# The first DeltaNet triangular solve in pinned pieces inside the attention, its row steps on GpSimd; weight splits pinned one projection ahead

## The chip, the cores and the metric

The kernel runs on one core of a Trainium2 chip. The metric is the device time of one execution in microseconds (us); for the kernel before, the median of three runs is 1260.77 us (1259.69 to 1261.77). The core's engines are TensorE (PE, matrix products, PEld its weight loads), VectorE (DVE), ScalarE (ACT), GpSimd (POOL) and SyncE (SP), whose queue issues the DMAs. Each works through its own instructions in order and waits on semaphores for the others.

## The reference

One layer of a hybrid transformer on 512 latent tokens with 256 context tokens, width 1024, in float32. One input projection feeds two branches, which are gated, merged, projected and followed by a gated MLP:

```python
attn_x = latent_attention(q_x, k_all, v_all)          # 8 query heads, 2 key heads, 768 keys
gdn_x_in = gdn_prepare(qkv_x, db_x, da_x, conv_qkv_w, a_log, dt_bias)   # conv, silu, l2 norm, rates
o_x, o_c = gdn_bidirectional(gdn_c_in, gdn_x_in, update_ctx)            # 8 heads, both directions
gdn_x = gdn_output(o_x, z_x, gdn_norm_w)
x = x + g1 * merge_branches(attn_x, gdn_x, gate_x, w_pa, w_pd, w_out)
x = x + g2 * conv_ffn(modulate(rms_norm(x), sh2, sc2), w_up, ffn_conv_w, ffn_conv_b, w_down)
```

The change is in the DeltaNet branch. In each chunk of 64 tokens it solves a triangular system per head and direction:

```python
a_mat = jnp.where(strict, beta[..., :, None] * dec * kk, 0.0) + jnp.eye(GDN_CHUNK)
uw = lax.linalg.triangular_solve(a_mat, rhs, left_side=True, lower=True, unit_diagonal=True)
```

Here kk are the products of keys with keys, dec the decays between two tokens and beta a rate per token. The kernel inverts a_mat: first its diagonal blocks of 32 by substitution, then larger blocks by products.

## The kernel before, in words

**Products.** A float32 matrix is split into a high and a low part (`split`: ACT writes whi, DVE writes wlo = wraw - whi, L121), and a product is three matmuls (hi·hi, hi·lo, lo·hi; `mm3`, L125). A weight block is fetched by `load_w` (L200): a DMA on SP into wraw (128x1024), then its split.

**Stages.** Up to 75 us the modulation vectors. To about 153 us the attention's q, k and v columns: `pq` in PSUM, rotary steps on DVE (qt, qtmp), transposes `pt`. Then the attention (`attend`, L824): 32 units, each a head with 128 queries. A unit's scores go to the PSUM tile pS; DVE takes the maximum (mx, a TENSOR_REDUCE), ACT the exponential (pm), DVE normalises, PE transposes pm into the bank ab, ACT and DVE split that into PH and PL, and PE multiplies with the values. PE's waits in a unit are filled with steps of the DeltaNet input projections (`projections`, L419: matmuls mb, taps t1 and output co on ACT and DVE, transposes xb). From 326.86 us DeltaNet is done for four pairs of heads, while what is left of the projections, the gates and the attention's output projection serves as filler (`filler`, L1201). What of the filler is left behind the last scan runs then; the output projection, up and down follow.

**DeltaNet of a pair.** `gdn_prep` (L875) loads the keys kT and, broadcast from DRAM, decays (NN and Gb), adds a mask (768 columns at a time) and takes 24 exponentials on ACT. `gdn_solve` (L903) multiplies 12 products of keys (bank pk) into NN, collects the diagonal blocks by transposes and ACT copies into C, transposes C into X, scales it with the rates gT and does the substitution: for each of 31 rows one product (prod) and one addition into R. `gdn_solved` (L940) scales R by gT and transposes it into o_tr and o_nt. `gdn_inv` (L952) begins with products pb of o_tr and o_nt with NN and builds the inverse T (tiles TTm, Tm), `gdn_scan` (L1020) runs over the chunks; its first matmul is pb with vtok. rkk and hk are inverse norms of keys and values; each of the eight heads has one rsqrt for each on GpSimd.

**What sets the order.** The scheduler orders each engine by priority (`first`, `sooner`, `solver`, `early`, L141 to 151); `keep_in_program_order` pins an instruction to its place in the program. PE's are pinned in this part, so no matmul passes another that waits. How much filler lies between DeltaNet steps is set by counts: `weave(g, rate)` takes `rate` steps of filler for each step of g, `wait(n)` is n steps with no DeltaNet work. WK = 24 steps stand ahead of the first solve, W0 = 66 behind it; `both(inv, solve)` weaves the next pair's solve into an inversion. The first solve runs on DVE, the other three on GpSimd (SPOOL).

Of the kernel before, what the change touches and what calls it, by code (L numbers as in the profile page):

```python
# [31 lines left out]
CHUNK, WK, W0, W1, RI, RS, RO = 1, 24, 66, 0, 3.0, 2.8, 2.0  # L32
# [34 lines left out]
RA = .6  # L67
F0, F1, F2, F3 = 3, 1, 1, 1
# [9 lines left out]
def hybrid_layer_body(tc, x, ctxt, xT, consts, cols, rows, w_mod1, w_mod2, w_av, w_aq, w_cm, w_pa, w_pd, w_out,  # L78
# [26 lines left out]

    def tt(out, a, b, op, eng=None):
        (eng or V).tensor_tensor(out=out, in0=a, in1=b, op=op)  # L107

    def ts(out, a, s1, op0, s2=None, op1=None, eng=None):
        if op1 is None:  # L110
            (eng or V).tensor_scalar(out=out, in0=a, scalar1=s1, scalar2=None, op0=op0)
        else:
            (eng or V).tensor_scalar(out=out, in0=a, scalar1=s1, scalar2=s2, op0=op0, op1=op1)  # L113

    def stt(out, a, s, b, op0, op1):
        V.scalar_tensor_tensor(out=out, in0=a, scalar=s, in1=b, op0=op0, op1=op1)  # L116

    def act(out, a, f=AF.Copy, **kw):
        A.activation(out, a, f, **kw)  # L119
# [13 lines left out]
    with es:  # L133
# [89 lines left out]
        vtd = [dp.tile([P, NA], F32, name=f"vtd{i}") for i in range(NH)]  # L223
        szd = [dp.tile([P, NL], F32, name=f"szd{i}") for i in range(NH)]
# [54 lines left out]
        def conv_proj(tile_idx, out, with_ctx):  # L279
            w = load_w(w_cm[tile_idx])  # L280
# [58 lines left out]
        def head_proj(h, part):  # L339
            o = cbuf()  # L340
            yield from conv_proj(8 * part + h, o, part != 0)
            head_out(h, part, o)
# [325 lines left out]
        QH = [ap_.tile([P, 2, NL], F32R, name=f"QH{i}") for i in range(4)]  # L668
        QL = [ap_.tile([P, 2, NL], F32R, name=f"QL{i}") for i in range(4)]
        kv_es = ExitStack()  # L670
        with kv_es:
# [27 lines left out]

            pend, dec = [], decays(kvp)  # L700
            pinned[0] = KPIN
            psc = next(dec)
            for blk in range(6):
# [5 lines left out]
                for t in range(6 if blk < 2 else 4):  # L709
# [10 lines left out]
                    if len(pend) >= LAG:  # L720
                        columns(*pend.pop(0))
# [27 lines left out]
                if blk > 1:  # L749
# [10 lines left out]
        with at_es:  # L760
# [13 lines left out]
            def abank():  # L774
                return aps.tile([P, 512], F32, name="ab", tag="ab", bufs=NB - 2)

            hold = {}
# [33 lines left out]
            def softmax(h, t, pS):  # L811
# [3 lines left out]
                with sooner():  # L815
                    V.tensor_reduce(out=mx[:, 0:1], in_=pS[:, 0:NA], axis=AX.X, op=ALU.max)
                    stt(mx[:, 1:2], mx[:, 0:1], -1.0, sc, ALU.mult, ALU.mult)
                    act(pm, pS[:, 0:NA], AF.Exp, scale=sc, bias=mx[:, 1:2], accum_out=mx[:, 2:3])
                with first():
# [3 lines left out]

            def attend():  # L824
                U = 4 * NH
                at = lambda u: (u // 4, u % 4)
                pS, pms, pv = scores(0, 0), {}, None
                yield F0
                for u in range(U + 2):
                    if u < U:  # L830
                        pms[u] = softmax(*at(u), pS)
                    if u + 1 < U:
                        pS = scores(*at(u + 1))
                    yield F1
# [360 lines left out]

        with early():
            pre = gdn_prep(0, V if P0 else G)
# [3 lines left out]
        def filler():  # L1201
# [4 lines left out]
            for h in range(NH):  # L1206
                yield from head_proj(h, 0)
                ready.append(h)
                yield from z_proj(h)
# [109 lines left out]
        weave(gdn_solve(pre, G if 0 in SPOOL else V), RK)  # L1319
        gdn_solved(pre, False)  # L1320
# [8 lines left out]
        for p in range(NP):  # L1329
            cur = pre  # L1330
            pre = gdn_prep(p + 1) if p + 1 < NP else None
            g = stage(p, cur, pre)
            weave(g, RI if p else RI0)
# [275 lines left out]
```

## Time and profile before

| | us |
|---|---|
| median of three runs | 1260.77 |
| profiled execution | 1257.86 |
| its span, first to last instruction | 1256.0 |
| attention's first scores | 156.27 |
| filler behind the attention begins | 326.86 |
| first inversion (pb<-o_tr) | 420.06 |
| first matmul of scan 0 (pb<-vtok) | 447.95 |
| second inversion | 511.61 |

The 1.86 us between execution and span lie outside the first and last instruction. Times of the profile are counted from the span's start. A row names the engine, the line of the kernel (often that of a helper), the operation, the output and input tiles with their sizes, how many it groups, and the busy time; in brackets or behind the last bar stands the idle time before it and what ended it.

### The profile page before, as it was taken

The numbers are of one execution on the slowest core, as the hardware profiler recorded it, in microseconds if no ns is written. First come the engines' busy times: TensorE is split into PE (matmuls) and PEld (weight loads), VectorE is DVE, ScalarE is ACT, GpSimd is POOL, SyncE is SP. The second block draws the span as 40 slices with busy tenths as digits, with TensorE's granted clock in tenths as the row PEclk, the third lists the DMA queues.
The fourth block names the chain that finished last, engine by engine and source line by source line (L and its number), as shares of the span: only waits on it lengthen the run. The fifth ranks groups of instructions, "written<-read, shape, count | busy, mean of one in ns | idle before, by whom it ended". The sixth has DMA issues, their size and how long they took to land.

```text
span 1256.0 us, 20509 instructions
## 1 busy us (share of the span) xinstructions
PE 1194.4 (95%) x7733; PEld 1016.6 (81%) x7733; DVE 837.5 (67%) x1609; ACT 613.3 (49%) x1403; POOL 274.3 (22%) x347
## 2 busy tenths in 40 slices
PE   6999999999888899999999999999999999999996
PEld 3499879898777778778888678789888888888886
DVE  5766767777688867775757688855776756653333
ACT  6534466666675673673643622333544444442231
POOL 0020110110432488587484200210000000000000
PEclk9999999999999999999999999999999999999998
DMA  9312211211634443543536786764343333223331
GB/s 381 140 59 85 88 58 59 81 59 68 201 110 171 159 134 114 165 155 105 173 135 193 241 288 198 274 215 135 96 138 121 132 101 101 91 90 99 99 93 67
DMA packets 66403, 171.83 MB, mean 137 GB/s; under 512 B 7328, under 2 KB 18048, under 8 KB 64896
## 3 DMA queue, kind: packets, MB, share of 16 engines
q1 hardware_dynamic: 66304, 170.52, 40.4%
q8 instruction: 61, 1.00, 0.3%
q14 instruction: 38, 0.31, 0.1%
HBM read 145.28 MB, written 25.21 MB: 136 GB/s over the span
## 4 chain that ended last, share of the span: by engine, by line
PE 75%; DVE 8%; DMA 6%; POOL 4%; ACT 3%; issue 2%; SPq 0%; POOLq 0%; DVEq 0%; ACTq 0%
PE mc L86 33%; PE mb L86 19%; PE pq L86 6%; PE pb L86 5%; PE pS L86 3%; PE ab L86 3%; PE pm L86 2%; PE ab L90 2%; DVE wlo L107 2%; DMA NN<-gamdr 1%; DMA wl<-in_w_mod_dram 1%; POOL prod L107 1%; PE pk L86 1%; POOL R L107 1%; PE xb L90 1%
## 5 line engine op out<-in xcount | busy, mean ns | idle before, releaser
L107 DVE TENSOR_TENSOR wlo<-wraw,whi 128x1024 fp32r<-128x1024 f32 (+1 forms) x153 | 192.0, 1256 | 152.7 <-ACT whi L119 152.1
L119 ACT ACTIVATE whi<-wraw 128x1024 fp32r<-128x1024 f32 (+1 forms) x153 | 159.6, 1044 | 218.4 <-PE mc L86 112.4
L86 PE MATMUL mc<-h,whi 128*128 128x512 f32 (+1 forms) x752 | 219.5, 376 | 0.3 <-ACT whi L119 0.3
L86 PE MATMUL mb<-hxH,whi 128*128 128x512 f32 x384 | 161.3, 420 | 5.9 <-DVE t L116 3.8
L86 PEld LDWEIGHTS mc<-h,whi 128*128 128x128 f32 x752 | 138.0, 188 | 26.0 <-ACT whi L119 0.5
L86 PE MATMUL mb<-hxH,wlo 128*128 128x512 f32 x384 | 151.2, 394 | 0.0
L86 PE MATMUL mb<-hxL,whi 128*128 128x512 f32 x384 | 150.7, 392 | 0.0
L86 PE MATMUL mc<-h,wlo 128*128 128x512 f32 (+1 forms) x376 | 141.3, 376 | 0.5 <-DVE wlo L107 0.5
L86 PE MATMUL mc<-a,whi 128*128 128x512 f32 (+1 forms) x396 | 111.1, 366 | 0.6 <-DVE x L116 0.6
L107 POOL TENSOR_TENSOR rc<-rc,mhalf 128x2 f32<-128x2 f32 x4 | 3.0, 742 | 407.8 <-DVE rc L113 407.8
L86 PEld LDWEIGHTS mb<-hxH,whi 128*128 128x128 f32 x384 | 72.9, 190 | 16.3 <-ACT t L119 4.5
L86 PEld LDWEIGHTS mb<-hxH,wlo 128*128 128x128 f32 x384 | 72.3, 188 | 16.5
L86 PEld LDWEIGHTS mc<-a,whi 128*128 128x128 f32 x396 | 71.5, 189 | 13.0 <-DVE x L116 0.8
L86 PEld LDWEIGHTS mc<-h,wlo 128*128 128x128 f32 x376 | 70.8, 188 | 13.7 <-DVE wlo L107 1.0
L86 PEld LDWEIGHTS mb<-hxL,whi 128*128 128x128 f32 x384 | 72.9, 190 | 9.5
L86 PE MATMUL mc<-a,wlo 128*128 128x512 f32 (+1 forms) x198 | 72.3, 365 | 0.0
L116 DVE SCALAR_TENSOR_TENSOR u<-mc,col,u 128x511 f32<-128x511 f32 x88 | 65.4, 747 | 1.4
L107 POOL TENSOR_TENSOR prod<-X,R 128x31 f32<-128x31 f32 (+15 forms) x93 | 54.2, 583 | 20.7 <-DVE X L107 13.9
L107 POOL TENSOR_TENSOR R<-R,prod 128x31 f32<-128x31 f32 (+15 forms) x93 | 57.1, 614 | 7.0
L86 PE MATMUL pq<-whi,hxH 128*128 128x256 f32 (+1 forms) x192 | 55.5, 289 | 0.0
L86 PE MATMUL pq<-wlo,hxH 128*128 128x256 f32 (+1 forms) x192 | 54.4, 283 | 0.1
L86 PE MATMUL pq<-whi,hxL 128*128 128x256 f32 (+1 forms) x192 | 54.2, 282 | 0.0
(329 smaller groups left out, 2769.5 us busy)
## 6 DMA issues: line engine op xcount, KB each, us to landing
wraw<-in_w_cm_dram SPq DMA_DIRECT2D x48, 512.0 KB, 3.5
wraw<-in_w_up_dram SPq DMA_DIRECT2D x44, 512.0 KB, 3.3
wl<-in_w_mod_dram SPq DMA_DIRECT2D x24, 512.0 KB, 4.3
wm<-in_w_mod_dram SPq DMA_DIRECT2D x8, 1024.0 KB, 10.6
wraw<-in_w_down_dram SPq DMA_DIRECT2D x16, 512.0 KB, 3.6
wraw<-in_w_aq_dram SPq DMA_DIRECT2D x10, 512.0 KB, 3.8
M<-gamdr SPq DMA_DIRECT2D x64, 64.0 KB, 4.5
wraw<-in_w_pa_dram SPq DMA_DIRECT2D x8, 512.0 KB, 4.5
```

Source lines behind the costliest of these rows:

```text
L86: i = nc.tensor.matmul(*a, **k)
L90: i = nc.tensor.transpose(*a, **k)
L107: (eng or V).tensor_tensor(out=out, in0=a, in1=b, op=op)
L116: V.scalar_tensor_tensor(out=out, in0=a, scalar=s, in1=b, op0=op0, op1=op1)
L119: A.activation(out, a, f, **kw)
```

## The change

The first pair's solve leaves the part behind the attention and becomes `first_solve`, a list of pieces that `solve_pieces(u)` places in attention units, pinned to their places on each engine:

- units 2 to 18: the decays of pair 0 and its rates, masks now added on GpSimd, exponentials two at a time on ACT, the two directions added on GpSimd; the gram products of the first head in units 9 and 10. NN[1] and kT lie in sA, the blocks C, X and R in sB, both in buffers of queries (tag "Q") whose heads are finished;
- units 19 and 20: grams of the second head; units 21 to 24: the diagonal blocks, by half-size transposes on DVE and ACT copies; unit 25 the turn of C into X, unit 26 the scaling;
- from unit 27: all 62 row steps on GpSimd, and then the scaling of R (`close`, 128x1024) on GpSimd too.

NN goes to DRAM in unit 25 (2 x 384 KB), R behind `close` (512 KB); `gdn_first` reloads R, NN and kT behind the attention into the tiles that the inversion uses. There o_tr and o_nt are made with part 1 of `gdn_solved`, WK is 8 and W0 is 12, and `gdn_prep(1)` stands ahead of the first inversion. Pair 1's solve is no longer woven into that inversion, but follows it after W2 = 24 steps, before scan 0.

Beside this: a projection's weights are loaded and split in pinned places during the one before it (LA, LB, LN); the rsqrt of the last queries' norms (qsc[3]) is placed in attention units 1 and 2; the first pt and ab banks of PSUM are taken earlier; filler goes q, q, z, z instead of q, z per head.

```diff
-CHUNK, WK, W0, W1, RI, RS, RO = 1, 24, 66, 0, 3.0, 2.8, 2.0
+S0E, S0R, W2 = 2, 1, 24
+CHUNK, WK, W0, W1, RI, RS, RO = 1, 8, 12, 0, 3.0, 2.8, 2.0
+LA, LB, LN = 8, 1, 16
...
         def projections(i0, i1):
             for i in range(i0, i1):
-                yield from head_proj(*order[i])
+                for n, _ in enumerate(head_proj(*order[i], ahead.pop(i, None))):
+                    if n == (LA if i < KV else LB) and i + 1 < LN:
+                        ahead[i + 1] = in_order(load_w, proj_w(i + 1))
+                    yield
...
-                        columns(*pend.pop(0))
+                        columns(*pend.pop(0), *(pt1.pop() for _ in pt1[:]))
...
-                if blk > 1:
+                if 1 < blk < 5:
                     rsqrt(qsc[blk - 2], qsc[blk - 2], 1.0 / HD, EPS)
                     ts(qsc[blk - 2], qsc[blk - 2], HD ** -0.5, ALU.mult)
...
+                def gram(hh, c0, n):
+                    pb = xbank()
+                    for i in range(n):
+                        sl = slice((c0 + i) * P, (c0 + i + 1) * P)
+                        mm(pb[:, i, :], kT[hh][:, sl], kT[hh][:, sl])
+                    tt(NN[hh][:, c0:c0 + n, :], NN[hh][:, c0:c0 + n, :], pb[:, 0:n, :], ALU.mult)
...
+                def blocks(b, hh):
...
+                    C, sb = R[0], slice(32 * b, 32 * b + 32)
+                    put(V.transpose(C[sb, :, 12 + 6 * hh:18 + 6 * hh].rearrange("p j u -> p u j"), NN[hh][sb, :, sb]))
+                    act(C[sb, :, 6 * hh:6 * hh + 6], NN[hh][sb, :, sb].rearrange("p u j -> p j u"))
...
+                def row(j):
+                    m, n = 31 - j, j + 1
+                    pv = Gb.rearrange("p a b -> p (a b)")[:, 0:m * n].rearrange("p (i k) -> p i k", k=n)
+                    tt(pv, X[0][:, j, j + 1:32].unsqueeze(2).to_broadcast([P, m, n]),
+                       R[0][:, j:j + 1, 0:n].to_broadcast([P, m, n]), ALU.mult, G)
+                    tt(R[0][:, j + 1:32, 0:n], R[0][:, j + 1:32, 0:n], pv, ALU.add, G)
...
+                def close():
+                    tt(R[0], R[0], gT.unsqueeze(2).to_broadcast([P, 32, 32]), ALU.mult, G)
+                    SP.dma_start(rrd, R[0].rearrange("p a b -> p (a b)"))
...
+            def solve_pieces(u):
+                left = S0R
+                while left > 0:
+                    if not fnext:
+                        fnext.append(next(fs_, None))
+                    if fnext[0] is None or fnext[0][0] > u:
+                        return
+                    left -= fnext[0][1]
+                    in_order(fnext.pop()[2])
...
+        def gdn_first():
...
+            SP.dma_start(flat(R), rrd)
+            for hh in range(2):
+                SP.dma_start(flat(NN[:, 6 * hh:6 * hh + 6, :]), nnd[hh])
+                SP.dma_start(kT[:, hh, :], kTd[hh])
+            return [kT, None, NN, R]
...
         weave(wait(WK), 1.0)
-        weave(gdn_solve(pre, G if 0 in SPOOL else V), RK)
-        gdn_solved(pre, False)
+        gdn_solved(pre, False, 1)
+        second = gdn_prep(1)
         weave(wait(W0), 1.0)
...
+            if p == 0:
+                pre = second
+                weave(gdn_inv(p, cur), RI0)
+                weave(wait(W2), 1.0)
+                weave(gdn_solve(pre, G if 1 in SPOOL else V), RK)
+            else:
+                pre = gdn_prep(p + 1) if p + 1 < NP else None
+                weave(stage(p, cur, pre), RI)
```

**DVE, ahead of the attention's first maximum, before.** pq is the projection in PSUM, qt and qtmp its rotary steps, wlo weight splits of later projections, qsc the query scale:

```order
L107 TENSOR_TENSOR QL2_728<-pt_1883,QH2_724 128x2x128
L107 TENSOR_TENSOR qt_1888<-qt_1888,qtmp_1889 128x256
L107 TENSOR_TENSOR wlo_2159<-wraw_2157,whi_2158 128x1024
L107 TENSOR_TENSOR wlo_2402<-wraw_2400,whi_2401 128x1024
L107 TENSOR_TENSOR qt_1928<-pq_1898,qA_736 128x256
L107 TENSOR_TENSOR qtmp_1929<-pq_1898,qB_737 128x2x32 x4
L113 TENSOR_SCALAR qsc3_176<-qsc3_176 128x8
L107 TENSOR_TENSOR QL3_729<-pt_1923,QH3_725 128x2x128
L107 TENSOR_TENSOR qt_1928<-qt_1928,qtmp_1929 128x256
L111 TENSOR_SCALAR qsc3_176<-qsc3_176 128x8
L816 TENSOR_REDUCE mx_1975<-pS_1950 128x1
```

The same place after, up to the same maximum:

```order
L120 TENSOR_TENSOR Q_727<-pt_1882,Q_727 128x2x128
L120 TENSOR_TENSOR qt_1887<-qt_1887,qtmp_1888 128x256
L120 TENSOR_TENSOR qt_1927<-pq_1897,qA_735 128x256
L120 TENSOR_TENSOR qtmp_1928<-pq_1897,qB_736 128x2x32 x4
L120 TENSOR_TENSOR Q_728<-pt_1922,Q_728 128x2x128
L120 TENSOR_TENSOR qt_1927<-qt_1927,qtmp_1928 128x256
L841 TENSOR_REDUCE mx_1972<-pS_1947 128x1
```

Both weight splits and both qsc3 steps have left this place; the last rotary steps follow each other. Q_727 and Q_728 are the buffers that held QH and QL.

**GpSimd, from the end of the attention on, before.** C, R and TTm, Tm are tiles of the solve and the inversion; NN_4747 and Gb_4748 belong to pair 1:

```order
L107 TENSOR_TENSOR rkk4_181<-rkk4_181,mhalf_78 128x6
L107 TENSOR_TENSOR hk4_168<-hk4_168,col_74 128x6
L922 MEMSET C_4161 128x32x8
L866 MEMSET TTm_3891 128x3072
L866 MEMSET Tm_3892 128x768
L107 TENSOR_TENSOR rkk5_182<-rkk5_182,mhalf_78 128x6
L107 TENSOR_TENSOR hk5_169<-hk5_169,col_74 128x6
L107 TENSOR_TENSOR NN_4747<-NN_4747,cst_72 128x768 x2
L107 TENSOR_TENSOR Gb_4748<-Gb_4748,cst_72 128x768
L927 MEMSET R_4174 128x1024
L928 MEMSET R_4174 128x32
L107 TENSOR_TENSOR NN_4747<-NN_4747,Gb_4748 128x768
```

After, from the 29th of the 31 rows to the first use of o_tr; sB is R, Gb0 the product, gs0 the rates:

```order
L120 TENSOR_TENSOR Gb0_1987<-sB_3291 128x87
L120 TENSOR_TENSOR sB_3291<-sB_3291,Gb0_1987 128x3x29
L120 TENSOR_TENSOR Gb0_1987<-sB_3291 128x60
L120 TENSOR_TENSOR sB_3291<-sB_3291,Gb0_1987 128x2x30
L120 TENSOR_TENSOR Gb0_1987<-sB_3291 128x31
L120 TENSOR_TENSOR rkk5_185<-rkk5_185,mhalf_78 128x6
L120 TENSOR_TENSOR sB_3291<-sB_3291,Gb0_1987 128x31
L120 TENSOR_TENSOR hk5_172<-hk5_172,col_74 128x6
L120 TENSOR_TENSOR sB_3291<-sB_3291,gs0_1988 128x1024
L1018 MEMSET TTm_4054 128x3072
L1018 MEMSET Tm_4055 128x768
L1122 COPY TTm_4054<-o_tr_4113 32x12x32 x4
```

The row steps of the solve are new on GpSimd; rkk5 and hk5 now stand among the last of them (rkk4 and hk4 behind the 20th), and the scaling by gs0 closes the solve. Pair 1's masks come behind all this.

**SP and PE behind the attention, after.** SP, from the last store of an attention output on (rrd and nnd are the DRAM copies of R and NN, wraw weights of later projections):

```order
L833 DMA atd7_161<-ao_3847 128x512
L332 DMA ktd5_132<-co_4096 128x768
L928 DMA rrd_145<-sB_3291 128x1024
L1352 DMA R_4062<-rrd_145 128x1024
L1354 DMA NN_4061<-nnd0_143 128x768
L1355 DMA kT_4060<-kTd0_111 128x768
L219 DMA wraw_4430<-in_w_cm_dram 128x1024
L1354 DMA NN_4061<-nnd1_144 128x768
L1355 DMA kT_4060<-kTd1_112 128x768
L219 DMA wraw_4577<-in_w_cm_dram 128x1024
L1030 DMA kT_4117<-kTd2_113 128x768
```

The load of R follows its store on the same queue, and the keys, NN and further weights follow both. PE, at the first inversion after:

```order
L88 MATMUL mb_4215<-hxH_199,wlo_4079 128x512
L88 MATMUL mb_4215<-hxH_199,whi_4078 128x512
L88 MATMUL mb_4215<-hxL_643,whi_4078 128x512
L88 MATMUL mb_4215<-hxH_199,wlo_4079 128x512
L88 MATMUL pb_4246<-o_tr_4113,NN_4061 32x32
L88 MATMUL pb_4247<-o_nt_4114,NN_4061 32x32
L88 MATMUL pb_4248<-o_tr_4113,NN_4061 32x32
L88 MATMUL pb_4249<-o_nt_4114,NN_4061 32x32
```

Between the attention's last product with values and this place PE has 48 filler matmuls of 512 columns, 24 of 256 and six transposes after, 357 filler matmuls before; between the same point and scan 0 it is 339 after and 423 before (84 matmuls of 512 columns fewer, which now stand behind the last scan).

More of the change, by code (lines that the diff above doesn't have):

```diff
@@ L1205, in filler @@
             gpool.append(ge.enter_context(tc.tile_pool(name="gp", bufs=1, reuse_waits="tile")))
[L1206 to L1209, printed above, removed]
+            for h in range(0, NH, 2):
+                for i in range(2):
+                    yield from head_proj(h + i, 0)
+                    ready.append(h + i)
+                for i in range(2):
+                    yield from z_proj(h + i)
             for c in range(2 * KT - GL):
```

133 lines of the change are left out of this document (115 added, 18 removed).

## The prediction

> **What bounds the kernel now.** I read the page first, then the windows of TensorE (PE) by stage, then the PE timeline at the idle places, then the groups of the engines that release it. The page gives each engine's busy time and share of the span.
>
> ```profile
> span 1256.0 us, 20509 instructions
> PE 1194.4 (95%) x7733; PEld 1016.6 (81%) x7733; DVE 837.5 (67%) x1609; ACT 613.3 (49%) x1403; POOL 274.3 (22%) x347
> ```
>
> PE is the bound, and every matmul that the change touches is only moved. So the time can change only by PE's loss: idle time and time at a reduced clock. The next rows are stretches of 25 us; the columns are the stretch, PE, PEld, DVE, ACT and POOL busy, the granted clock, and the DMA share with GB/s.
>
> ```profile
> 150.00:175.00 25.00, 20.14 (x121) 17.10 (x120) 15.98 (x40) 14.11 (x43) 3.23 (x3) 0.93 0.17 58
> 250.00:275.00 25.00, 25.00 (x176) 22.83 (x174) 19.06 (x38) 16.18 (x41) 3.47 (x2) 1.00 0.14 50
> 325.00:350.00 25.00, 20.70 (x115) 18.07 (x115) 15.82 (x46) 17.28 (x58) 11.27 (x6) 0.94 0.68 221
> 350.00:375.00 25.00, 20.98 (x128) 17.78 (x127) 21.96 (x35) 16.21 (x38) 7.87 (x6) 0.99 0.35 117
> 375.00:400.00 25.00, 21.13 (x120) 18.48 (x119) 22.44 (x48) 15.84 (x51) 9.18 (x6) 0.93 0.42 148
> 400.00:425.00 25.00, 20.92 (x191) 17.14 (x189) 23.64 (x41) 17.38 (x46) 12.01 (x15) 0.94 0.53 172
> ```
>
> The attention (250 to 275) leaves PE no gap. The four stretches from 325 to 425 do: 100 - 83.73 = 16.3 us idle, and the clock shares lack 0.20 x 25 = 5.0 us, 21.3 in all. There DVE is at 22 to 23.6 of 25. The timeline of PE at the places that matter (start, duration, then the idle time before it and its releaser):
>
> ```profile
> 156.27 0.76 PE L86 MATMUL pS<-KH,QH 128*128 128x512 f32 x1 [3.02 <-DVE qsc L113]
> 326.86 0.40 PE L86 MATMUL mb<-hxH,whi 128*128 128x512 f32 x1
> 337.96 0.51 PE L86 MATMUL mb<-hxH,whi 128*128 128x512 f32 x1 [1.76 <-DVE t L116]
> 338.77 0.40 PE L86 MATMUL mb<-hxH,whi 128*128 128x512 f32 x1
> 343.35 0.39 PE L86 MATMUL mb<-hxH,wlo 128*128 128x512 f32 x1
> 346.99 1.11 PE L90 MATMUL xb<-cst,co 128*128 128x128 f32 x4 [2.54 <-DVE co L116]
> 413.27 0.44 PE L90 MATMUL xb<-cst,co 128*128 128x128 f32 x2 [2.11 <-ACT co L119]
> 437.98 0.71 PE L86 MATMUL pk<-kT 128*128 128x128 f32 x4
> 511.61 0.24 PE L86 MATMUL pb<-o_tr,NN 32*32 32x32 f32 x2 [1.01 <-DVE oacc L116]
> ```
>
> The stalls after 326.86 are filler whose taps or split (t, co) stand behind the first solve on DVE. What the solve puts there, from the DVE groups between 325 and 430:
>
> ```profile
> L107 DVE TENSOR_TENSOR prod<-X,R 128x31 f32<-128x31 f32 (+15 forms) x31 | 14.3, 462 | 0.6
> L107 DVE TENSOR_TENSOR R<-R,prod 128x31 f32<-128x31 f32 (+15 forms) x31 | 11.9, 384 | 0.6
> L920 DVE STREAM_TRANSPOSE C<-NN 32x384 f32<-32x384 f32 x4 | 3.6, 892 | 0.1
> L950 DVE STREAM_TRANSPOSE o_tr<-R 128x1024 f32<-128x1024 f32 x1 | 2.0, 2041 | 0.0
> L950 DVE STREAM_TRANSPOSE o_nt<-R 128x1024 f32<-128x1024 f32 x1 | 1.9, 1937 | 0.0
> ```
>
> The 62 row operations alone are 14.3 + 11.9 = 26.2 us. All of this except the last two transposes leaves DVE's stretch behind the attention.
>
> **The change part by part.** I add up changes of PE's loss.
>
> *1. Start of the attention.* DVE ahead of the first scores, before:
>
> ```profile
> 152.63 1.23 DVE L107 TENSOR_TENSOR wlo<-wraw,whi 128x1024 fp32r<-128x1024 f32 x1 [0.29 <-ACT whi L119]
> 155.52 0.61 DVE L107 TENSOR_TENSOR qtmp<-pq,qB 128x64 f32<-128x64 f32 x4
> ```
>
> This weight split and a second one right behind it hold up the rotary steps that empty pq. The change takes both splits and the qsc[3] step from this place. Left of the 3.02 us are perhaps 0.7 to 1, as long as the two rotary steps take. The stretch 150 to 175 lacks 0.07 of its clock, 1.75 us, which belongs to this stall and goes with it. Bounds -4.8 and 0; I take -4. (A rule differs: the Trainium skill, "TensorE: Matmul & The Clock Gate", Part 1, has the clock drop after at least one idle window of about 3.4 us. This stall of 3.02 us cost clock all the same; by the page alone the term would be an estimated -2.3.)
>
> *2. Pieces inside the attention.* They add 24 exponentials and 8 block copies on ACT, and on DVE the blocks, grams' products, turn and scaling. Their durations, from the ACT and DVE groups between 325 and 430:
>
> ```profile
> L119 ACT ACTIVATE NN<-NN,gam 128x128 f32<-128x128 f32 x24 | 7.6, 397 | 0.8 <-DVE NN L107 0.8
> L119 ACT ACTIVATE C<-NN 32x384 f32<-32x384 f32 x4 | 3.5, 886 | 0.0
> L107 DVE TENSOR_TENSOR NN<-NN,pk 128x512 f32<-128x512 f32 (+1 forms) x5 | 2.9, 578 | 3.2 <-PE pk L86 3.2
> L107 DVE TENSOR_TENSOR X<-X,gT 128x1024 f32<-128x1024 f32 x1 | 1.2, 1224 | 0.0
> ```
>
> ACT gets 24 x 0.397 + 3.5 = 13 us, DVE 3.6 + 4 x 0.58 + 2 x 1.2 = 8.3 us, spread over some 125 us in which DVE is busy 19 of 25 and ACT 16. They hide in those gaps, with the projections as PE's filler. Without that cover each of 25 units would wait for a piece of 0.4 to 0.9 us ahead of its own exponential or PL; at a quarter of that it is 2.5 to 5.6 us. I take +1, bounds 0 and +6. The 12 gram products move from behind the attention into it: no loss either way, but they shift its end by about 3 us (24 records, of which four take 0.71 us at 437.98: 4.3 at most, less where they overlap).
>
> *3. Behind the attention.* The inversion of pair 0 moves from behind 357 filler matmuls to behind 72 (48 of 512 columns, 24 of 256). Twenty-one matmuls of 512 start from 338.77 to 343.35, 0.229 us each; those of 256 are taken at half. So PE comes to it 11.0 + 2.8 + 0.7 (six transposes, of which four take 1.11 at 346.99 at a reduced clock) + about 2 (the wait that 337.96 shows) after the attention's end, at 326.86 - 4 + 1 + 3 = 326.9: at about 343.4.
>
> When is R there? GpSimd's groups: the rows of the fourth pair's solve (stretch 630 to 673), then its rsqrt pieces (160 to 340), then its 768-wide operations (326.8 to 448).
>
> ```profile
> L107 POOL TENSOR_TENSOR R<-R,prod 128x31 f32<-128x31 f32 (+15 forms) x31 | 18.5, 597 | 2.4
> L107 POOL TENSOR_TENSOR prod<-X,R 128x31 f32<-128x31 f32 (+15 forms) x31 | 17.9, 579 | 16.3 <-DVE X L107 13.9
> ...
> L107 POOL TENSOR_TENSOR rkk<-rkk,mhalf 128x6 f32<-128x6 f32 x6 | 10.2, 1701 | 157.4 <-ACT rkk L119 157.4
> L107 POOL TENSOR_TENSOR hk<-hk,col 128x6 f32<-128x6 f32 x6 | 8.4, 1393 | 0.0
> ...
> L107 POOL TENSOR_TENSOR NN<-NN,Gb 128x768 f32<-128x768 f32 x2 | 4.7, 2330 | 3.0 <-ACT Gb L119 3.0
> ```
>
> The 62 rows take 18.5 + 17.9 + 2.4 + (16.3 - 13.9) = 41.2 us on GpSimd, start to end, against 26.2 on DVE. (The Trainium skill, "GPSIMD Engine Reference", 4.1, puts GpSimd at about 2x slower than VectorE for two-input elementwise work; the rows show 1.57x for these small shapes. By the page it would be an estimated 52 us; rival B says what that makes of the time.) Two pairs rkk, hk stand among the rows: 2 x (1.70 + 1.39) = 6.2. The closing multiply over 1024 columns, from the 768-wide 2.33 and less for the calmer shapes: 2.8 (bounds 2.5 and 3.1).
>
> The rows start when X is scaled, placed on DVE just ahead of the 28th of 32 score maxima. Before, that and the DMAs were:
>
> ```profile
> 295.61 0.96 DVE L816 TENSOR_REDUCE mx<-pS 128x1 f32<-128x768 f32 x1 [0.60 <-PE pS L86]
> ...
> wraw<-in_w_cm_dram SPq DMA_DIRECT2D x48, 512.0 KB, 3.5
> vtd<-co SPq DMA_DIRECT2D x8, 384.0 KB, 2.7
> kT<-kTd SPq DMA_DIRECT2D x8, 384.0 KB, 6.3
> ```
>
> 295.6 - 4 + 1 + 3, and about 1 for the scaling itself less the idle 0.60: rows from 296.5. Then 41.2 + 6.2 + 2.8, the store of R to DRAM 2.7, its load back 3.5 (behind the store on SP's queue, with the NN and kT loads and the next weights queued behind it; those weights are wanted only later), and o_tr and o_nt 2.0 + 1.9: the inversion can start at 356.8. PE's order is fixed, so it stands idle 356.8 - 343.4 = 13.4 us, and then pays the clock: 1.75 us as in part 1. That is 15.2 us of new loss. Bounds of the stall: 7 (rows from 295.6, smaller close and DMAs, only o_tr waited for: ready 353, PE there at 346) and 27 (rows from 298.5, five us of interference with DVE, loads at 6.3: ready 368.6, PE there at 342).
>
> Of the old 21.3 us of loss here I keep 5: the wait at 337.96, ACT's at 413.27, and one spell of clock. The rest waited for DVE work that is gone. So this stretch goes from 21.3 to 20.2: -1. The 84 filler matmuls taken out of it run later, at full rate: 0.
>
> *4. Later.* Pair 1's solve now stands between the first inversion and scan 0, with the masks of M2 among its rows on GpSimd; the second inversion's waits (1.01 at 511.61 and 1.7 behind it in the same burst) may shrink, or grow when that R is late. -1, bounds -4 and +4.
>
> Sum: -4 + 1 - 1 - 1 = -5 us. The profiled execution took 1257.86 us (span 1256.0 and 1.9 outside), so 1252.9; the runs' median is 1260.77, 2.9 above it, and what I forecast is compared with that: **1255.8 us**.
>
> **The rivals.**
> - *A, R comes early* (0.22). The stall behind the attention is near its lower bound 7, and the leftover loss 3 instead of 5: 8 to 9 us better, 1247. For it: the attention has slack on DVE, and DMAs outside bursts are short. Against: rows, rsqrt pieces, close, store, load and transposes are one chain, each from a row.
> - *B, slower* (0.16): R comes late at the first inversion. GpSimd's rows lie beside DVE's two-input work and the bounce through DRAM beside the stretch where the DMA share is 0.68; every microsecond is PE idle, since nothing may pass. At the upper bound of 27 it is 13.6 worse than forecast, 1269; it decides the sign from a stall of 18.4 on, the inversion later than about 362, and the 0.2% from 21 on. One way to it alone: rows at twice DVE's 26.2 us, 52.4, are 11.2 longer, 1267; the 41.2 of the fourth pair leaves that 0.03 of the chance. (That is the Trainium skill's rule of part 3, "GPSIMD Engine Reference", 4.1.)
> - *C, no change* (0.12): the attention pays 0.2 us in each of 25 units (+5), through pieces placed on ACT and DVE ahead of its exponentials. For it: ACT waits for DVE's mx in each unit, so the chain is short of slack. Then 1260.8. The same comes out if the first stall of part 1 stays: pq still has to be emptied.
>
> **How the numbers follow.** The forecast case has 0.50. About 0.2% (2.5 us) is what a measurement of this kernel can tell from no change: 1258.3 to 1263.3 is "same". The forecast case lies mostly below it (0.47 of 0.50), A wholly: faster 0.69. C and the edge of the forecast: same 0.15. B: 0.16. The range leaves out the best end of A, where all lower bounds meet (-21 us, 1240), and the upper half of B: 1243 to 1264.
>
> **What would show it.** Right: pS about 3 us earlier with little idle before it; no idle in the attention; rows on GpSimd from about 296 to 344; one idle block of 7 to 20 us on PE ahead of pb<-o_tr, released by o_tr or o_nt, with a lower clock behind it; DVE below 20 of 25 between 360 and 420; scan 0 (pb<-vtok) some 20 us earlier, the tail longer by as much less the gain. Wrong: that block absent or over 20 us, the attention itself longer than before beyond the 3 us of grams, or new waits at the second inversion that eat more than 4 us.

## The result, and the profile after

| | before | changed |
|---|---|---|
| median of the runs | 1260.4 us | 1278.5 us (1271.5 to 1283.0, 4 runs) |
| ratio to before, 95% interval | | 1.0141, 1.0114 to 1.0168 |
| profiled execution; its span | 1257.86; 1256.0 | 1271.51; 1269.7 |

The change costs 18 us; 5 us of gain was forecast. The profiled execution of the changed kernel is the fastest of its four, so I also read a second one of the same kernel (run g4_after, 1276.8 us, span 1275.0). Spans of the stages in us, from the PE timelines:

| profiled execution | first scores at | attention | its end to first inversion | to scan 0 | scan 0 to output projection | from there |
|---|---|---|---|---|---|---|
| before | 156.3 | 170.6 | 93.2 | 27.9 | 385.7 | 422.3 |
| changed | 151.0 | 183.6 | 25.8 | 77.8 | 408.9 | 422.7 |
| changed, g4_after | 153.6 | 183.6 | 26.8 | 79.6 | 408.1 | 423.4 |
| e1, no pinned splits | 153.7 | 181.8 | 19.8 | 74.8 | 411.8 | 422.5 |
| i1, pins but no rows | 153.9 | 183.5 | 18.9 | 74.1 | 405.3 | 423.6 |

From the attention's end to scan 0 before takes 121.1 us; with 19.2 (84 matmuls of 0.229) and the 2.6 of the grams moved away, equal loss would be 99.3; the changed kernel takes 103.5 and 106.4. (The grams' 24 records start 0.11 us apart in e1's trace, hence 2.6.) The attention is 13 us longer, 2.6 of it the grams; behind scan 0, 4 us go beyond the 19.2 (7 in e1).

A part of the 13 us is only that the first scores come earlier. A fixed point ahead of them is the third-last rotary step that reads pq on DVE, here in the kernel before, the changed kernel and g4:

```profile
147.77 0.42 DVE L107 TENSOR_TENSOR qt<-pq,qA 128x256 f32<-128x256 f32 x1 [1.33 <-ACT qtmp L119]
145.74 0.42 DVE L120 TENSOR_TENSOR qt<-pq,qA 128x256 f32<-128x256 f32 x1 [1.33 <-ACT qtmp L132]
148.33 0.42 DVE L120 TENSOR_TENSOR qt<-pq,qA 128x256 f32<-128x256 f32 x1 [1.33 <-ACT qtmp L132]
```

From this point to the attention's end it is 179.1 us before and 188.9 in both executions of the changed kernel, 9.8 longer, of which 7.2 are not the grams. In e1 it is 187.1 (from 148.46). Where "from the rotary step" stands below, this measure is meant; it leaves out how late an execution came to the attention.

The page of the changed kernel, first lines:

```profile
span 1269.7 us, 20524 instructions
PE 1192.6 (94%) x7733; PEld 1015.9 (80%) x7733; DVE 811.9 (64%) x1544; ACT 614.6 (48%) x1407; POOL 319.5 (25%) x416
```

PE has the same work as before in a span 13.7 us longer; DVE is relieved by 25.6 us, GpSimd loaded by 45. The windows, columns as in the prediction:

```profile
150.00:175.00 25.00, 21.02 (x130) 17.57 (x129) 18.27 (x41) 16.36 (x52) 7.86 (x5) 1.00 0.25 69
175.00:200.00 25.00, 22.16 (x153) 19.86 (x152) 17.75 (x34) 18.06 (x48) 2.61 (x2) 1.00 0.24 80
250.00:275.00 25.00, 24.10 (x167) 21.80 (x166) 19.24 (x48) 16.49 (x45) 2.89 (x3) 1.00 0.19 64
350.00:375.00 25.00, 18.78 (x285) 15.62 (x285) 15.61 (x35) 10.79 (x26) 15.39 (x16) 0.81 0.66 243
375.00:400.00 25.00, 21.38 (x174) 18.10 (x174) 10.87 (x14) 21.41 (x65) 10.16 (x7) 0.94 0.46 155
425.00:450.00 25.00, 20.97 (x110) 16.86 (x109) 14.92 (x22) 19.15 (x56) 21.66 (x34) 1.00 0.63 190
```

Before, the second of these stretches was:

```profile
175.00:200.00 25.00, 24.11 (x166) 21.65 (x165) 18.35 (x36) 17.93 (x49) 3.65 (x3) 1.00 0.17 64
```

The attention has more gaps than before (22.16 where 24.11 stood, 24.10 where 25.00 stood). Between 350 and 400 DVE has fallen to 15.6 and 10.9 of 25, and PE still loses 10 us of time and 6 of clock there. DVE's load is no longer the reason for PE's waits, yet they remain. PE's timeline shows which:

```profile
155.68 0.51 PE L88 MATMUL pS<-KH,Q 128*128 128x512 f32 x1 [1.30 <-ACT pm L132]
195.45 0.50 PE L88 MATMUL pS<-KH,Q 128*128 128x512 f32 x1 [1.54 <-ACT pm L132]
334.60 0.40 PE L88 MATMUL mb<-hxH,whi 128*128 128x512 f32 x1
348.92 0.56 PE L88 MATMUL mb<-hxH,wlo 128*128 128x512 f32 x1 [4.51 <-DVE wlo L120]
360.35 0.28 PE L88 MATMUL pb<-o_tr,NN 32*32 32x32 f32 x2 [4.53 <-DVE o_tr L1102]
391.05 0.52 PE L92 MATMUL xb<-cst,co 128*128 128x128 f32 x3 [1.81 <-DVE co L129]
438.12 0.38 PE L88 MATMUL pb<-vtok,TTm 128*128 128x128 f32 x2
```

Three kinds: scores waiting for an exponential (the one at 195.45 recurs about once per projection), a filler matmul waiting for its low split, and the inversion waiting for R. First a unit with such a wait, on DVE and then on ACT:

```profile
189.20 1.54 DVE L129 SCALAR_TENSOR_TENSOR t<-mb,col,t 128x511 f32<-128x511 f32 x2 [0.28 <-ACT t L132]
190.65 1.22 DVE L120 TENSOR_TENSOR wlo<-wraw,whi 128x1024 fp32r<-128x1024 f32 x1
191.78 0.95 DVE L841 TENSOR_REDUCE mx<-pS 128x1 f32<-128x768 f32 x1
...
194.33 0.98 ACT L132 ACTIVATE pm<-pS,mx,qsc 128x768 f32<-128x768 f32 x1
```

The pinned wlo stands between the taps and the unit's maximum, so the maximum starts at 191.78 although PE had finished those scores by about 191. There is one pS, so the next scores wait for the exponential. Another pinned split stands ahead of the scaling of X, for which the rows wait (in e1, without it, the scaling starts at 300.21):

```profile
300.26 1.22 DVE L120 TENSOR_TENSOR wlo<-wraw,whi 128x1024 fp32r<-128x1024 f32 x1
...
302.12 1.22 DVE L120 TENSOR_TENSOR sB<-sB,gs 128x1024 f32<-128x1024 f32 x1
```

Next, R's chain on GpSimd (first and last rows, rkk and hk, close) and DVE behind the attention:

```profile
303.81 0.24 POOL L120 TENSOR_TENSOR Gb<-sB 128x31 f32<-128x31 f32 x1 [5.91 <-DVE sB L120]
...
346.23 1.33 POOL L120 TENSOR_TENSOR rkk<-rkk,mhalf 128x6 f32<-128x6 f32 x1
347.53 0.25 POOL L120 TENSOR_TENSOR sB<-sB,Gb 128x31 f32<-128x31 f32 x1
347.74 2.31 POOL L120 TENSOR_TENSOR hk<-hk,col 128x6 f32<-128x6 f32 x1
350.03 1.91 POOL L120 TENSOR_TENSOR sB<-sB,gs 128x1024 f32<-128x1024 f32 x1
```

```profile
346.62 0.96 DVE L129 SCALAR_TENSOR_TENSOR co<-co,t 128x768 f32<-128x768 f32 x1 [0.96 <-ACT co L132]
347.49 0.15 DVE L124 TENSOR_SCALAR gwh<-col 128x1 f32<-128x1 f32 x1
347.56 2.44 DVE L120 TENSOR_TENSOR wlo<-wraw,whi 128x1024 fp32r<-128x1024 f32 x2
...
358.34 1.91 DVE L1102 STREAM_TRANSPOSE o_tr<-R 128x1024 f32<-128x1024 f32 x1 [5.99 <-DMA R<-rrd]
360.10 1.95 DVE L1102 STREAM_TRANSPOSE o_nt<-R 128x1024 f32<-128x1024 f32 x1
```

The rows start 7.3 us later than forecast (296.5), and close ends at 351.9. The first split behind the attention stands on DVE behind the output co of the projection before it, which is why PE waits 4.51 us while DVE has little to do.

### The profile page after: what moved, and what is told of

The parts are those of the page before. It is cut to its first block, busy times and chain, and to the rows that moved or that the text cites. A ratio compares the mean times of both kernels' runs of the same rounds, so it can differ in the third digit from the quotient of the medians.

```text
span 1269.7 us, 20524 instructions
## 1 busy us (share of the span) xinstructions
PE 1192.6 (94%) x7733; PEld 1015.9 (80%) x7733; DVE 811.9 (64%) x1544; ACT 614.6 (48%) x1407; POOL 319.5 (25%) x416
## 5 line engine op out<-in xcount | busy, mean ns | idle before, releaser
L88 PE MATMUL mb<-hxH,whi 128*128 128x512 f32 x384 | 164.0, 427 | 6.7 <-DVE t L129 5.3
L88 PEld LDWEIGHTS mc<-h,wlo 128*128 128x128 f32 x376 | 70.8, 188 | 13.8 <-DVE wlo L120 1.0
L129 DVE SCALAR_TENSOR_TENSOR t<-mb,col,t 128x511 f32<-128x511 f32 (+1 forms) x76 | 49.0, 647 | 24.8 <-ACT t L132 23.8
```

The source lines that it names most:

```text
L88: i = nc.tensor.matmul(*a, **k)
L129: put(V.scalar_tensor_tensor(out=out, in0=a, scalar=s, in1=b, op0=op0, op1=op1))
```

## The experiments

Two theories stood at first: P, the pinned splits cost the time by standing ahead of the attention's maxima; S, the solve's pieces do. Eighteen runs followed in five groups; each group shares one chip and its runs of before. Ratios are to the kernel before.

**Pins.** The edits are one constant (the names of runs in the code cuts are added here), and for e5 the hunks of the diff on `load_w`, `ahead` and `projections` in the kernel before.

```diff
-LA, LB, LN = 8, 1, 16
+LA, LB, LN = 8, 1, 0       # e1; e2: 8, 1, 10; e3: -1, 1, 16; f2: 8, 1, 4
```

> The changed kernel without the pinned weight splits (LN = 0: each projection loads its own weights, unpinned, as before). Theory P (the pinned splits stand on ACT and DVE ahead of the attention's maxima and exponentials, once per projection, 1.7 us each): the time from the first scores to the filler falls from 183.6 to about 172 us, the pS waits on pm disappear, the 4.7 us wait for wlo behind the attention too; about 1264 us, 1259 to 1269. Theory S (the pieces of the solve do it: exponentials on ACT, blocks on DVE): the attention stays at 181 to 184 us and the time within 4 us of 1278.

> The changed kernel with the splits pinned for the attention's projections only (LN = 10). Theory P: attention still 182 to 184 us, the wlo wait behind it gone: about 1272 us. Theory S: the same here, about 1273, so this run only prices the pins of the filler (5 us by the wlo wait; 0 if that wait moves to the first inversion, which then waits for R all the longer).

> The changed kernel with the splits pinned for the filler's projections only (LA = -1). Theory P: attention about 172 us, the wlo wait stays: about 1268 us. Theory S: attention 181 to 184 us, about 1278.

> The kernel before with the pinned weight splits alone added (LA, LB, LN = 8, 1, 16), its solve where it was. Theory P: attention from 170.5 to about 181 us, less up to 4 us because the two splits ahead of the first scores are gone: about 1268 us, 1264 to 1274. Theory S: attention as before, 1257 to 1261.

| run | median us | ratio, interval | attention |
|---|---|---|---|
| e1 | 1267.4 | 1.0060, 1.0033 to 1.0087 | 181.8 |
| e2 | 1278.6 | 1.0166, 1.0108 to 1.0223 | 185.9 |
| e3 | 1270.0 | 1.0083, 1.0057 to 1.0109 | 181.2 |
| e5 | 1272.1 | 1.0102, 1.0063 to 1.0142 | 172.7 |

The pins of the attention's projections cost 8 to 11 us (e2, e3, e1), those of the filler nothing that these runs separate. But P has the wrong place: without pins the attention is still 181.8, not 172, and in the kernel before the pins leave it at 172.7. There they cost time behind the attention, by another in-order queue:

```profile
349.04 0.80 PE L87 MATMUL mb<-hxH,whi 128*128 128x512 f32 x1 [13.82 <-DVE NN L119]
```

In e5 PE stands 13.8 us before the filler whose split is on DVE behind the solve's masks and rates, which wait for loads and GpSimd. In e1 the wait for wlo is gone, and R's chain closes 5.7 us earlier than in the changed kernel, 9.4 earlier than in g4 (GpSimd, first row and close; rkk and hk of the last head now come behind close):

```profile
301.57 0.24 POOL L120 TENSOR_TENSOR Gb<-sB 128x31 f32<-128x31 f32 x1 [3.23 <-DVE sB L120]
...
344.32 1.92 POOL L120 TENSOR_TENSOR sB<-sB,gs 128x1024 f32<-128x1024 f32 x1
346.19 2.40 POOL L120 TENSOR_TENSOR rkk<-rkk,mhalf 128x6 f32<-128x6 f32 x1
```

e2 shows where the price lies. Its pins end with the attention's projections, so the first filler's split is not pinned, and PE has no wait for wlo behind the attention. It costs as much as all the pins all the same, because R is late (PE and GpSimd):

```profile
366.08 0.28 PE L88 MATMUL pb<-o_tr,NN 32*32 32x32 f32 x2 [11.94 <-DVE o_tr L1102]
```

```profile
355.75 1.91 POOL L120 TENSOR_TENSOR sB<-sB,gs 128x1024 f32<-128x1024 f32 x1
```

The close starts 11.4 us later than in e1, and PE waits 11.94 us for o_tr against 4.93 in e1. Of the 12.4 us by which e2 reaches scan 0 later than e1, 4.1 are the attention and 7.0 the way from there to the inversion. (e2's profiled execution is 10 us above its median, but it reaches scan 0 at 442.5, g4 at 443.6; what it loses more lies behind.) So the wait for wlo in the changed kernel is not needed for the price: R was not there either way.

**Placement, on e1's base.** f3 takes the filler's order q, z per head back from before.

```diff
-                    in_order(fnext.pop()[2])
+                    fnext.pop()[2]()                 # f1
...
-CHUNK, WK, W0, W1, RI, RS, RO = 1, 8, 12, 0, 3.0, 2.8, 2.0
+CHUNK, WK, W0, W1, RI, RS, RO = 1, 8, 24, 0, 3.0, 2.8, 2.0    # f4
```

> As e1 (no pinned splits), and the pieces of the solve no longer pinned on DVE, ACT and GpSimd (they may float by priority; PE's order is unchanged). Theory S2 (what is left of the longer attention, 181.7 us against 170.5 with 3 of it for the moved grams, comes from pinned pieces in front of the unit's own exponential): the attention falls by 3 to 6 us; the solve ends later or as early; about 1263 us. Rival (it is the work itself, ACT and DVE being short in each unit, wherever the pieces stand): attention within 1.5 us of 181.7, 1266 to 1269.

> The changed kernel with weight splits pinned for the first two projections inside the attention only (LN = 4). If the pins help at the attention's start, where they take two splits away from the first scores (first exponential at 154.5 us in the changed kernel, 158.7 in e1, 159.8 before), and hurt in its units: first exponential by 155, attention's later pS waits as in e1, about 1264 us. Rival (start and end of the attention don't sum: the gain at the start is lost in the next unit): 1267.

> As e1, with the filler's order q, z per head as before in place of q, q, z, z. Theory: the 3.6 us wait of the transposes xb on ACT's squares near 530 us, with its spell of clock, comes from two q projections in a row; it goes, and the stretch from scan 0 to the first product of the output projection loses 3 to 5 us of its 412: about 1263. Rival (the wait is of the projection before it, or the time comes back in the next wait): 1266 to 1268.

> As e1, with W0 = 24 in place of 12: about 50 more matmuls of filler ahead of the first inversion. If the idle time ahead of it (4.9 us and a spell of clock, 7 in all) is R's chain on GpSimd and DRAM, it is filled and the time falls by 5 to 7: about 1261. Rival (R isn't the limit, or scan 0 and the second pair's solve then start late and the loss shows there): 1266 to 1268.

f1: 1273.0 (1.0110, 1.0083 to 1.0138), attention 192.2: floating pieces hurt more than pinned ones, both theories of that run miss. f2: 1268.5 (1.0077, 1.0049 to 1.0106), as e1: from the rotary step its first exponential comes 1.4 us earlier than e1's (8.8 against 10.2 us), and its attention ends 0.1 earlier (186.9 against 187.1). The pins near the start gain nothing. f3: 1272.8 (1.0106, 1.0082 to 1.0130): the wait near 530 goes (second inversion to scan 1 34.2 us against 37.0), but first inversion to scan 0 takes 82.2 against 74.8; the new order is good for this weave. f4: 1270.5 (1.0097, 1.0061 to 1.0133): more filler ahead of the inversion buys nothing. Why, in f4's PE row and DVE rows:

```profile
359.66 0.77 PE L88 MATMUL mb<-hxH,whi 128*128 128x512 f32 x1 [5.96 <-DVE t L129]
```

```profile
355.20 1.90 DVE L1102 STREAM_TRANSPOSE o_tr<-R 128x1024 f32<-128x1024 f32 x1 [3.08 <-DMA R<-rrd]
356.97 1.96 DVE L1102 STREAM_TRANSPOSE o_nt<-R 128x1024 f32<-128x1024 f32 x1
358.81 0.70 DVE L129 SCALAR_TENSOR_TENSOR t<-mb,col,t 128x511 f32<-128x511 f32 x1
```

The inversion no longer waits, but the filler does: its taps stand behind o_tr, which waits for R's load. Filler cannot cover a wait that stands in the queue of an engine the filler needs.

**What in the solve costs, on e1's base.** g1 leaves out the exponentials, g2 the rows, h2 the work on DVE and PE; g3 sets S0R = 2; h1 leaves out pair 1's exponentials behind the attention.

```diff
-                    for c in (c0, c0 + 1):
-                        kc = rows6(d, hh).start + c
-                        act(D[:, c, :], D[:, c, :], AF.Exp, scale=-1.0, bias=gam[:, kc:kc + 1])
+                    put(G.memset(D[:, c0:c0 + 2, :], 0.0))     # g1
...
-                for j in range(31):
+                for j in range(0):                             # g2; i1: the same in the changed kernel
...
-S0E, S0R, W2 = 2, 1, 24
+S0E, S0R, W2 = 2, 2, 24                                        # g3
...
-                    for c in range(6):
+                    if p == 1:
+                        G.memset(D, 0.0)
+                    for c in range(6 if p != 1 else 0):        # h1, in gdn_prep
...
-                        mm(pb[:, i, :], kT[hh][:, sl], kT[hh][:, sl])
-                    tt(NN[hh][:, c0:c0 + n, :], NN[hh][:, c0:c0 + n, :], pb[:, 0:n, :], ALU.mult)
...
-                    put(V.transpose(X[0].rearrange("p a b -> p (a b)"), R[0].rearrange("p a b -> p (a b)")))
+                    put(G.memset(X[0], 0.0))                   # h2; its block copies and scaling go too
```

> As e1 (no pinned splits), with the 24 exponentials of the solve's decays left out of the attention (12 clears of 256 columns on GpSimd stand in their places; the solve works on zeros, and the output is not the reference's). Theory A (the attention lengthens because ACT's 9.5 us of exponentials stand in the units' chain): attention from 181.8 to 176 to 178 us, time 3 to 6 us below e1. Rival D (DVE's blocks, turn, scaling and products do it): attention within 1.5 us of 181.8.

> As e1, with the 62 row operations on GpSimd left out (R stays the identity, the output is not the reference's); the rest, with its store and load of R, stays. Theory: R is there 40 us earlier, the idle time of about 5 us ahead of the first inversion with its spell of clock goes: 5 to 8 us below e1. If GpSimd's rows also slow DVE in the attention (their operations overlap its last five units), the attention falls too, by 1 to 2. Rival (the wait at the inversion only moves to the taps behind it, DVE being short): within 2 us of e1.

> As e1, with up to two pieces in a unit (S0R = 2): the rows start some seven units earlier. Theory: R is ready at about 320 us plus store and load, well ahead of the inversion; DVE's queue behind the attention isn't held by o_tr any more: 5 to 8 us below e1, about 1260. Rival (two pieces in a unit cost the attention more than one): attention 3 us or more longer, time as e1 or above.

> As e1 (no pinned splits), with pair 1's 24 exponentials left out of the part behind the attention (clears of 768 columns on GpSimd in their places; pair 1 solves zeros, the output is not the reference's). Theory A1 (ACT is the limit between the first inversion and scan 0, as the filler of 121 us now runs in about 95 beside the same exponentials): that stretch falls from 75 to 66 to 70 us and the time by 5 to 9. Rival (the waits there are DVE's queue or DMAs): within 2 us of e1's 1267.

> As e1, with the solve's gram products, their multiplications into NN, the block transposes and copies, the turn and the scaling left out of the attention (X is cleared on GpSimd; the output is not the reference's). Theory D (these, not the exponentials, lengthen the units): attention from 181.8 to 173 to 176 us (2.6 of it the grams on TensorE), time 4 to 8 us below e1. Rival (the longer attention comes with the moved start: the first scores earlier, the same wait in the second unit): attention 178 to 179 us, that is the grams alone.

| run | median us | ratio, interval | attention |
|---|---|---|---|
| g1 | 1271.3 | 1.0087, 1.0053 to 1.0121 | 184.1 |
| g2 | 1266.2 | 1.0051, 1.0023 to 1.0079 | 181.8 |
| g3 | 1267.0 | 1.0063, 1.0042 to 1.0085 | 184.7 |
| h1 | 1273.6 | 1.0120, 1.0059 to 1.0182 | 181.9 |
| h2 | 1255.4 | 0.9975, 0.9944 to 1.0007 | 177.2 |

Leaving the exponentials out of the attention gains nothing (g1: its attention is 2.3 us longer than e1's). Without pins the rows are nearly free too (g2): the inversion no longer waits for o_tr, but PE waits 2.76 us for the filler's taps ahead of it instead. g3 brings the rows forward to 273, the stall goes and the attention pays for it. What costs are the solve's pieces on DVE and PE (h2): 11 us by the ratios, with 2.6 of PE's own work, of which 4.6 show in the attention; the rest is spread over the stages behind it and not assigned. (R is early in h2 too, which g2 prices at 1 us.)

h1 misses both its cases: it is 6 us above e1. ACT has 11 us less to do between 335.5 and 437 us (61.1 against 72.1), and the next pair's exponentials stand about where they stood, first e1, then h1:

```profile
378.20 0.40 ACT L132 ACTIVATE NN<-NN,gam 128x128 f32<-128x128 f32 x1
```

```profile
379.40 0.40 ACT L132 ACTIVATE NN<-NN,gam 128x128 f32<-128x128 f32 x1 [0.50 <-POOL NN L120]
```

Yet it takes 80.3 us from the first inversion to scan 0, against 74.8. So ACT's exponentials are not shown to limit that stretch; why it became longer stays open (the profiled execution is the slowest of h1's four).

**The start, and the filler's order, in the kernel before.** h4 takes over the banks `pt1`, `ab1` and the placing of qsc[3]; h3 and i2 are the order q, q, z, z alone.

```diff
-                if blk > 1:
+                if 1 < blk < 5:                   # h4, with the other hunks on pt1, ab1 and between
...
-            for h in range(NH):
-                yield from head_proj(h, 0)
-                ready.append(h)
-                yield from z_proj(h)
+            for h in range(0, NH, 2):             # h3, i2; f3 is the reverse
+                for i in range(2):
+                    yield from head_proj(h + i, 0)
+                    ready.append(h + i)
+                for i in range(2):
+                    yield from z_proj(h + i)
```

> The kernel before with the attention's start changed as in the changed kernel (earlier pt and ab banks, qsc[3] inside units 1 and 2) and nothing else. By the prediction's first term: 4 us faster. By what e1's trace shows (first scores 2.6 us earlier, but the second unit then waits 2.9 us for the first exponential, behind the same two splits on DVE): within 1.5 us of the kernel before.

> The kernel before with the filler's order q, q, z, z per two heads as the only change. If that order is worth time by itself, as f3 against e1 (1272.8 against 1267.4) suggests: 2 to 5 us below the kernel before, 1256 to 1258. Rival (it only suits the changed weave): within 2 us of 1260.5.

> The kernel before with the order q, q, z, z alone, again, in five rounds. If the order is worth its 2.6 us of h3: 1257 to 1259 with an interval below 1. If that was the spread between executions: within 1 us of the kernel before.

h4: 1260.5 against 1259.9 (1.0013, 0.9987 to 1.0040): these hunks are worth nothing. They leave the two splits where they were, so h4 tests only a part of the start; in f2 and e5 the splits are gone too. h4's first scores come 3.4 us earlier, and the second unit then stands:

```profile
152.87 0.48 PE L86 MATMUL pS<-KH,QH 128*128 128x512 f32 x1
...
159.05 0.80 PE L86 MATMUL pS<-KH,QH 128*128 128x512 f32 x1 [2.78 <-ACT pm L130]
```

h3: 0.9985 (0.9954 to 1.0015); i2: 0.9983 (0.9962 to 1.0005), 1256.3 against 1259.5. Both lie 2 to 3 us below before, each with 1 in its interval: no version came out that is shown to beat both kernels.

**Pins and rows together.**

> The changed kernel itself once more, beside these: 1275 to 1281 if the pins' price (e1 against the changed kernel, 11 us) holds on this chip; under 1272 would say that a part of it is a difference between executions.

> The changed kernel with all its pins, the 62 row operations on GpSimd left out (R stays the identity, the output is not the reference's); g2 is the same without the pins (1266.2). If the pins cost their 10 us through R's lateness: R is early here whatever the pins do, the price shrinks to the attention's 2 to 4 us, 1268 to 1271. If they cost by their own places (the wait for wlo behind the attention, the units' exponentials): 1274 to 1278.

g4: 1277.6 (1.0140, 1.0102 to 1.0179), the result again. i1: 1263.4 (1.0023, 1.0007 to 1.0039), 14 us below the changed kernel, and not above g2. So the pins cost nothing where R is early; their price needs the row chain. i1 at the inversion, on PE and DVE:

```profile
337.37 0.40 PE L88 MATMUL mb<-hxH,whi 128*128 128x512 f32 x1
356.23 0.21 PE L88 MATMUL pb<-o_tr,NN 32*32 32x32 f32 x1
```

```profile
338.93 1.23 DVE L120 TENSOR_TENSOR wlo<-wraw,whi 128x1024 fp32r<-128x1024 f32 x1 [1.21 <-ACT whi L132]
343.79 2.06 DVE L1102 STREAM_TRANSPOSE o_tr<-R 128x1024 f32<-128x1024 f32 x1 [2.46 <-DMA R<-rrd]
```

No wait for o_tr, and none for wlo: with the rows gone the scheduler also puts that split ahead of the taps. i1 alone does not separate R's lateness from this place; e2 does, where that wait is gone, R is late and the price is paid in full. Most of it behind the attention is thus R's lateness; 2 to 4 us are the attention's own (from the rotary step 188.9 in the changed kernel and 191.2 in e2, against 187.1 in e1).

## Why the prediction was wrong, point by point

- **That only PE's loss can change** held: PE's busy time is 1192.6 against 1194.4, and the difference is idle time and clock.
- **Where the 18 us are.** For g4, whose span is 19.0 us above before: 0.6 ahead of the attention, 7.2 for terms 1 and 2 together (forecast -3), 7.1 behind the attention (forecast -1), 4.1 later (forecast -1). The faster execution has -2.0, 7.2, 4.3 and 4.3, 13.7 in all.
- **Term 1, the start, -4:** the stall went, and the gain did not arrive. In the changed kernel no wait stands ahead of the first scores, the stretch 150 to 175 has a clock of 1.00, and from the rotary step the first exponential starts 3.3 us earlier than before (8.8 against 12.1 us). But this first wait was the first link of a chain, scores, maximum, exponential, next scores: 1.30 us of wait come at the second unit, and where the start was changed by itself nothing is left of the gain at the attention's end (from the rotary step 178.9 us in h4 and 179.8 in e5 against 179.1 before; 186.9 in f2 against 187.1 in e1). In h4 and e1 the maximum stays behind the two splits on DVE; in f2 and the changed kernel the splits are gone, and where in the attention the gain is lost there is not traced. Only the first of several waits in a row was priced.
- **Term 2, the pieces, +1:** mis-sized, and the step before the sum failed, "they hide in those gaps". Busy shares of 19 and 16 of 25 were taken for slack. With the start, the attention costs 7.2 us beside the grams, 5.4 without pins (e1). The forecast's rival C named this with 0.2 us a unit and 5 us, and an attention longer beyond the grams' 3 us was its sign of being wrong. The exponentials among the pieces are not the reason as far as g1 shows; the pieces on DVE and PE have 2 of it beside the grams (h2), the rest stays open.
- **Term 3, behind the attention, -1:** the parts held singly, the sum did not. On GpSimd the rows took 40.0 us (42.7 in e1 from first to last, with one head's rkk and hk among them) against 41.2; rkk and hk 1.3 each (2.3 once) against 1.4 to 1.7; close 1.9 against 2.8; store 2.6 and load 3.6 against 2.7 and 3.5. Without pins the stretch takes 94.6 us against 99.3 at equal loss, -4.7. With them it is 103.5 to 106.4, +4 to +7. Two things failed. The pins were costed at nothing beyond the start: they delay the scaling of X and so the rows, and the order puts rkk and hk ahead of close, so that R is late (e2: 11.94 us of wait). That one split also makes PE wait 4.5 us falls into the time in which R is not there. And "the rest waited for DVE work that is gone": the waits on co and t are still there with DVE idle (391.05), since those tiles come through ACT, DVE and back in a chain of its own, with other work queued in between.
- **The stall for R** was forecast at 13.4 and measured 4.5 to 5.7, with R later than forecast (360.3 and 364 against 356.8), because PE came later still, after an attention that ended late and 4.5 us of wait for wlo.
- **Term 4, later, -1:** +4, and +7 in e1. The wait near 530 belongs to the order q, q (f3); the rest is not assigned.
- **The rivals.** B put the slow outcome on R alone, from an inversion at 362. It came at 360.4 and 364, so that the point was about reached, but the 18 us are C's price and the lateness that the pins add on top; no rival joined them. The changed attention was not counted as making R late and PE late at once.
- **Its arithmetic.** By its own terms the rows start at 296.0, not 296.5 (295.6 - 4 + 1 + 3 + 1 - 0.6), and the terms named for the upper bound of R give 366.6, not 368.6 (356.8 + 2 + 5 + 2.8). DVE at 22 to 23.6 holds for three of the four stretches behind the attention; the first has 15.8. None of this turns the sign.
- **Two rules that the prediction named.** The Trainium skill, "TensorE: Matmul & The Clock Gate", Part 1, has the clock drop after an idle window of about 3.4 us. After the change the clock is at 0.81 in the stretch with stalls of 4.5 and 1.5 us; in e1 the stretch 150 to 175 stands at 0.93 with no gap above 2.7. Shorter gaps cost clock here. The Trainium skill, "GPSIMD Engine Reference", 4.1, would have made the rows an estimated 52 us; they took 40.0, so the forecast's own row was the better price.

## What to carry to other kernels

Before pieces are woven into a stage that keeps its bound engine full, follow the chain of one unit through the queue of every engine: a busy share says nothing about the place at which a piece stands. An instruction pinned into an in-order queue costs what waits behind it, and pays or hurts with its neighbours: the same pins were free in the changed kernel without its rows, and cost 10 us with them. And a wait that ends with an engine is not yet that engine's load; if the engine was idle before, what it waited for is the cause.

## What the runs showed of the hardware

Executions of one kernel on one chip differ by more than most of these edits: i2's twelve took 1250.6 to 1266.0 us, the changed kernel's four 1271.5 to 1283.0. In these two the mean granted clock goes along, 0.988 and 0.977 at i2's ends, 0.986 and 0.979 at the changed kernel's: 0.007 of 1277 us is 8.9 of those 11.5, an estimate that takes all the time to go with the clock. It is no rule: of i1's twelve, one took 1259.1 us at 0.985 and one 1264.8 at 0.988. That short gaps of PE make the spread is not shown. The attention itself hardly takes part: from the rotary step to its end the two executions of the changed kernel agree to 0.01 us, those of before, h3 and i2 to 0.1. A single profiled execution can be 7 to 10 us off its median (the changed kernel's, e2's).
